# A decoder layer's last stage: the closing norms given behind the last expert's down product, and two late sums kept in weight slots

## The chip, the core and the metric

The kernel runs on one core of one Trainium2 chip. The metric is the device time of one execution in microseconds; the number shown is the median of three runs. A core has five instruction queues that concern us: TensorE (PE in the rows), VectorE (DVE), ScalarE (ACT), GpSimd (POOL) and SyncE (SP). SP issues the plain DMA transfers, POOL issues the indirect ones (gathers and scatters of rows by a list of indices), and both run on the core's 16 DMA engines. Every engine takes its own instructions strictly in the order in which they stand.

## The reference, cut to what matters

One decoder layer over 1024 tokens of width 1024 (T = D = 1024), in float32: parallel token mixing, cross-attention, and then a mixture of 16 experts, each sublayer followed by a layer norm. Only the end of it matters here:

```python
y = grouped_moe(x, router_w, router_bias, moe_w_gate[l], moe_w_up[l], moe_w_down[l])
x = layer_norm(DN_ALPHA * x + y, ln3_g[l], ln3_b[l])

# in grouped_moe, for a block xb of 128 tokens of expert e
(jax.nn.silu(xb @ w_gate[e]) * (xb @ w_up[e])) @ w_down[e]
# every token has two experts; their outputs are weighted by the gate and summed per token
```

## The kernel before

`Experts.run` does the 16 experts, `NE = 16`, in an order that is drawn up at run time: eight of them (a fixed first one and the seven fullest) with a second, smaller block of up to 64 rows, and the emptiest two (`LATE = 2`) last. By place in that order they are experts 0 to 15 here, so 14 and 15 are the late ones, and expert 13 is the last that has a second block. An expert gathers 128 token rows (`gather`), turns them (`turned`), and multiplies them by its gate, up and down weights. All products are float32 in three passes: each operand is split into a high and a low part (`split`, line 28, and `parts`, lines 1533 and 1534: ACT writes the high part, DVE the low one) and `mm3` (lines 35 to 37) makes three matmuls of it. The products land in the PSUM banks `eacc`, the turned tokens in `etp`, the split hidden row block in `ehh` and `ehl`.

`accd` (`self.acc`) is a table in device memory of one row per token. It starts as the residual, already divided by the layer's factor, and every expert adds its weighted rows `ey` to it with an indirect DMA that accumulates (line 1642). The last layer norm turns it into the output, in two ways:

- **The tiles.** `tiles` loads the 1024 rows of `accd` as 8 tiles of 128 tokens (line 1778, on SP's queue, into four slots that otherwise hold raw weights, `wraw`, two tiles in a slot), takes the mean and variance of each (`moments`: on DVE by line 980, two instructions a tile, for tiles 0, 1 and 7; on ACT by lines 974 and 975 for tiles 2 to 6), gets the reciprocal root on POOL (lines 976, 982 and 983), applies them in two passes of DVE over 128x1024 (`apply`, lines 989 and 994), and stores each tile to `out` (line 1784).
- **The late experts.** Experts 14 and 15 don't wait for that. Each gathers its tokens' rows from `accd` into a buffer `z` (named `exg`), adds its own weighted down product to it on DVE (line 1639, one instruction for each half of the width), norms `z` in the same way, and scatters the finished rows to `out` over those that the tiles have written (line 1645). It also adds its rows to `accd`, since expert 15 may hold a token of expert 14, and since a loop behind the experts (`rest`, which does nothing with these inputs) reads `accd` again.

The experts are generators with four steps: turn the tokens, gate product, up product, down product with the outputs. `run` interleaves them; in round n it gives the gate product of expert n, then the down product of n-1, then the turning of n+1, then the up product of n. In round 15 the tiles stand between the first two:

```python
            step(n)
            if n == NE - LATE + 1:
                ...
                x = [self.piece("raw").rearrange("p (a b) c -> p a (b c)", a=2) for _ in range(HOLD)]
                self.tiles([x[t // 2][:, t % 2] for t in range(2 * HOLD)])
            step(n - 1)
```

That order is not yet the order on the engines. The program goes through a scheduler with a timing model of its own, which sets the order of every engine's queue and keeps the dependences; what is given earlier tends to come earlier. What one operation needs of another becomes a wait on a semaphore. DMAs of POOL signal on eight of them in turn, DMASW0 to DMASW7; those of SP on DMAHW0 to DMAHW7.

Of the kernel before, what the change touches and what calls it, by code (L numbers as in the profile page):

```python
# [7 lines left out]
F32 = mybir.dt.float32  # L8
# [3 lines left out]
ALU = mybir.AluOpType  # L12
# [1246 lines left out]
FIRST = (14, 6, 6, 6, 6, 6, 6, 7)  # L1259
HOLD = 4  # L1260
CUT, LOPOOL = 4, ()
LATE = 2
# [214 lines left out]
class Experts:  # L1477
# [20 lines left out]

    def piece(self, kind):
        s = self.slots[kind]  # L1500
        pool, tag = s[self.n[kind] % len(s)]
        self.n[kind] += 1
        return pool.tile([128, 4, 512], F32 if kind == "raw" else F32R, tag=tag, bufs=1, name="w" + kind)

# [9 lines left out]

    def load(self, e, i):
        a = self.k.a
        raw = self.piece("raw")
        w = a["moe_w_" + ("gate", "up", "down")[i // 2]][0]
        w = w[e:e + 1] if isinstance(e, int) else w[bass.ds(e, 1)]
        if i < 4:  # L1520
            w = w.rearrange("o (h c p) n -> h p (o c) n", h=2, p=128)[i % 2]
        else:
            w = w.rearrange("o (c p) (h n) -> h p (o c) n", h=2, p=128)[i % 2]
        self.k.nc.sync.dma_start(raw, w)
        return raw

    def parts(self, raw):
        nc = self.k.nc
        hi, lo = self.piece("hi"), self.piece("lo")
        n = 4 // CUT  # L1530
# [42 lines left out]

    def expert(self, px, ps, w, main, rem, first=None, late=False):


        k, nc = self.k, self.k.nc
        xh, xl = first or (px.tile([128, 8, 128], F32R, tag=n, bufs=2, name=n) for n in ("exh", "exl"))
        for q in range(0 if first else 2):
            k.split(self.turned(ps, main[2], q).rearrange("p (c t) -> p c t", c=4), xh[:, 4 * q:4 * q + 4], xl[:, 4 * q:4 * q + 4])  # L1580
        yield
        wt = w(0)
        o = self.bank(ps)
        for c in range(8):
            hi, lo = wt[c // 4]
            k.mm3(o, xh[:, c], xl[:, c], hi[:, c % 4], lo[:, c % 4], c == 0, c == 7)
        th = px.tile([128, 512], F32, tag="th", bufs=2, name="eth")
# [20 lines left out]
        for c in range(8):  # L1608
            hi, lo = wt[c // 4]
            k.mm3(o, xh[:, c], xl[:, c], hi[:, c % 4], lo[:, c % 4], c == 0, c == 7)  # L1610
# [4 lines left out]
        hh, hl = (px.tile([128, 4, 128], F32R, tag=n, bufs=1, name=n) for n in ("ehh", "ehl"))  # L1615
        wt = w(2, k.split(self.turned(ps, th, 0).rearrange("p (c t) -> p c t", c=4), hh, hl))
        if rem:
# [9 lines left out]

        def result(tag, x, mm):
            y = px.tile([128, D], F32, tag="y" + tag, bufs=2 if tag == "m" else 1, name="ey")
            if late:  # L1630
                z = self.gather(px, x[0][:, 1:2], tag, self.acc)
            for d in range(2):
# [5 lines left out]
                if late:  # L1638
                    nc.vector.scalar_tensor_tensor(z[:, ds], o, x[1], z[:, ds], ALU.mult, ALU.add)  # L1639
            for r in ([slice(0, 128)] if tag == "m" else [slice(0, 64), slice(64, 128)]):  # L1640
                ix = x[0][0:r.stop - r.start, 1:2]
                nc.gpsimd.indirect_dma_start(out=self.acc, out_offset=bass.IndirectOffsetOnAxis(ap=ix, axis=0), in_=y[r, :], in_offset=None, compute_op=ALU.add, bounds_check=T - 1, oob_is_err=False)  # L1642
            if late:
                self.ln(z)
                nc.gpsimd.indirect_dma_start(out=self.out, out_offset=bass.IndirectOffsetOnAxis(ap=x[0][:, 1:2], axis=0), in_=z, in_offset=None, bounds_check=T - 1, oob_is_err=False)
        result("m", main, lambda o, f, hi, lo: k.mm3(o, hh[:, f], hl[:, f], hi[:, f], lo[:, f], f == 0, f == 3))
        if rem:
# [28 lines left out]
    def run(self, px, ps):  # L1676
# [41 lines left out]
        def step(n):  # L1718
            if 0 <= n < NE:
                if n == len(gens):  # L1720
                    gens.append(self.expert(px, ps, lambda i, after=(): pair(n, i, after), *toks[n], first=None if n else self.x0, late=n >= NE - LATE))
                next(gens[n])
        open_(0)
        gather(0, 1)
        step(0)
        open_(1)
        for n in range(NE + 1):
            if n == NE - LATE + 1:
                self.held = HOLD
            step(n)  # L1730
            if n == NE - LATE + 1:
                row = lambda tag: px.tile([128, D], F32, tag=tag, bufs=1, name="e" + tag)
                self.norm(self.pl, row("xgr"), row("exr"), [row("gr"), row("yr")])
# [7 lines left out]
            if n + 1 < NE:  # L1741
                gather(n + 1, 1)
    def ahead(self, experts=range(FIXED)):

        while self.at < 6 * NE and len(self.pre) < len(self.slots["raw"]) - self.held and self.seq[self.at][0] < len(experts):
            n, i = self.seq[self.at]
            self.pre.append(self.load(experts[n], i))
            self.at += 1
# [174 lines left out]
```

## Time and profile before

| | |
|---|---|
| median of 3 runs | 1833.93 us (1832.9 to 1838.39) |
| profiled execution, its own time | 1839.95 us |
| its span, first to last instruction | 1838.1 us |
| PE busy | 1724.6 us (94%) |
| DVE busy | 1228.9 us (67%) |
| ACT busy | 845.0 us (46%) |
| POOL busy | 434.3 us (24%) |
| mean granted clock of TensorE | 0.97 |

Times in the rows are microseconds from the span's start. "Busy" counts work only: an engine that waits, issues a DMA or branches isn't busy. The whole kernel is a TensorE kernel; the change touches its last 60 us, where TensorE runs out of work.

### The profile page before, as it was taken

What the parts mean: (1) busy time and instruction counts of PE and PEld (TensorE: products, weight loads), DVE (VectorE), ACT (ScalarE), POOL (GpSimd) and SP (SyncE); (2) the same over time, 40 slices, a digit from 0 to 9 for tenths busy, and PEclk for the clock granted to TensorE, in tenths of its full rate; (3) what the DMA queues carried; (4) which work ended last, traced back from release to release, by engine and by line L of the source; (5) the groups of instructions that cost most, each with busy time, mean ns of one, the idle gap of its engine ahead of it and who ended that gap; (6) DMA issues with size and microseconds to landing.
All of it is one profiled execution on the core that took longest, in us unless ns stands there. A gap on an engine that the chain in (4) does not pass through costs nothing. (4 is left out here: it accounts for less than half of the span.)

```text
span 1838.1 us, 27269 instructions
## 1 busy us (share of the span) xinstructions
PE 1724.6 (94%) x9254; PEld 1409.2 (77%) x9254; DVE 1228.9 (67%) x2821; ACT 845.0 (46%) x1756; POOL 434.3 (24%) x639
## 2 busy tenths in 40 slices
PE   8999989999999999999999889999996999999992
PEld 6877767877688878787887668778885888888871
DVE  4336766787875212698996865557866677777786
ACT  4233313444333221598885431043304667667672
POOL 0002101110110000366673221100033323333214
PEclk9999989999999999999999999999978999999996
DMA  7364344454333238602104745214415999989974
GB/s 239 112 186 131 110 150 130 133 169 135 107 95 91 86 97 246 206 10 93 33 12 133 232 154 172 72 29 149 161 47 187 307 299 297 294 294 306 312 273 151
DMA packets 252798, 295.96 MB, mean 161 GB/s; under 512 B 63789, under 2 KB 150981, under 8 KB 252144
## 3 DMA queue, kind: packets, MB, share of 16 engines
q1 hardware_dynamic: 245184, 273.52, 45.4%
q0 software_dynamic: 7472, 20.67, 4.6%
q8 instruction: 74, 1.21, 0.3%
q14 instruction: 68, 0.56, 0.1%
HBM read 231.88 MB, written 70.98 MB: 165 GB/s over the span
## 5 line engine op out<-in xcount | busy, mean ns | idle before, releaser
L35 PE MATMUL acc<-xh,wh 128*128 128x512 f32 (+1 forms) x656 | 269.6, 412 | 3.8 <-ACT ev L240 1.4
L36 PE MATMUL acc<-xl,wh 128*128 128x512 f32 (+1 forms) x656 | 265.2, 405 | 0.0
L37 PE MATMUL acc<-xh,wl 128*128 128x512 f32 (+1 forms) x656 | 264.6, 404 | 0.0
L1534 DVE TENSOR_TENSOR wlo<-wraw,whi 128x512 fp32r<-128x512 f32 x384 | 237.5, 684 | 32.6 <-ACT whi L1533 27.9
L1533 ACT CAST whi<-wraw 128x512 fp32r<-128x512 f32 x384 | 206.0, 621 | 19.1 <-issue 17.8
L35 PEld LDWEIGHTS acc<-xh,wh 128*128 128x128 f32 (+1 forms) x656 | 123.1, 188 | 39.2 <-issue 5.6
L37 PEld LDWEIGHTS acc<-xh,wl 128*128 128x128 f32 (+1 forms) x656 | 123.4, 188 | 33.8 <-issue 5.9
L36 PEld LDWEIGHTS acc<-xl,wh 128*128 128x128 f32 (+1 forms) x656 | 123.4, 188 | 32.1 <-issue 5.5
L477 ACT ACTIVATE pp<-pp,nm 128x640 f32<-128x640 f32 (+7 forms) x128 | 94.1, 738 | 8.2 <-DVE nm L476 6.5
L28 DVE TENSOR_TENSOR pl<-ptp,ph 128x512 fp32r<-128x512 f32 x132 | 87.9, 685 | 13.3 <-ACT ph L28 12.6
L120 DVE TENSOR_TENSOR wl<-wraw,wh 128x512 fp32r<-128x512 f32 (+1 forms) x82 | 52.8, 682 | 62.0 <-ACT wh L117 61.5
L35 PE MATMUL eacc<-whi,exh 128*128 128x512 f32 x240 | 94.2, 392 | 0.0
L36 PE MATMUL eacc<-wlo,exh 128*128 128x512 f32 x240 | 93.9, 391 | 0.0
L37 PE MATMUL eacc<-whi,exl 128*128 128x512 f32 x240 | 93.9, 391 | 0.0
L482 POOL TENSOR_SCALAR pp<-pp,wgt 128x640 f32<-128x640 f32 (+7 forms) x128 | 88.4, 711 | 0.6
L910 ACT COPY state<-rseq 64x64 f32<-64x64 f32 x128 | 26.6, 208 | 122.5 <-PE rseq L906 108.7
L28 ACT CAST ph<-ptp 128x512 fp32r<-128x512 f32 x132 | 74.3, 582 | 17.1 <-PE ptp L536 16.1
L536 PE MATMUL ptp<-ident,pp 128*128 128x128 f32 x528 | 79.8, 275 | 1.3 <-DVE pl L28 1.1
L1642 POOL DMA_INDIRECT accd<-ey,ef x32 | 52.1, 1628 | 115.2 <-ACT whi L1533 50.6
L852 DVE TENSOR_TENSOR tinv<-xinv,ln 128x60 f32<-128x60 f32 (+24 forms) x248 | 54.0, 218 | 32.8 <-DMA ln<-ld 27.0
L536 PEld LDWEIGHTS ptp<-ident,pp 128*128 128x128 f32 x528 | 64.5, 141 | 14.6 <-DVE pl L28 2.8
L467 PE MATMUL sp<-nk,nq 128*128 128x320 f32 (+5 forms) x192 | 71.9, 377 | 3.6 <-DVE nm L476 2.1
(497 smaller groups left out, 4291.0 us busy)
## 6 DMA issues: line engine op xcount, KB each, us to landing
wraw<-in_moe_w_up SPq DMA_DIRECT2D x32, 1024.0 KB
wraw<-in_moe_w_gate SPq DMA_DIRECT2D x32, 1024.0 KB
wraw<-in_moe_w_down SPq DMA_DIRECT2D x32, 1024.0 KB
wraw<-in_w_in SPq DMA_DIRECT2D x40, 512.0 KB
sm<-ev SPq DMA_DIRECT2D x32, 256.0 KB
sr<-ev SPq DMA_DIRECT2D x28, 256.0 KB
skew<-skew SPq DMA_DIRECT2D x1, 4608.0 KB
xraw<-in_x SPq DMA_DIRECT2D x8, 512.0 KB
```

Of the source, the lines that this page charges most:

```text
L28: x = nc.scalar.copy(hi, src), (nc.gpsimd if by_pool else nc.vector).tensor_tensor(lo, src, hi.bitcast(F32), ALU.subtract)
L35: nc.tensor.matmul(out, ah, bh, start=start, stop=False)
L36: nc.tensor.matmul(out, ah, bl, start=False, stop=False)
L37: nc.tensor.matmul(out, al, bh, start=False, stop=stop)
L120: nc.vector.tensor_tensor(wl[:, cs], raw[:, cs], wh[:, cs].bitcast(F32), ALU.subtract)
L467: nc.tensor.matmul(sp[:, o], t["q"][:, i, qs], t["k", br, "h"][:, kk], start=True, stop=False)
L477: nc.scalar.activation(pt[:, :n], pt[:, :n], AF.Exp, bias=nm, scale=-1.0, accum_out=sums[:, 0, i:i + 1])
L482: nc.gpsimd.tensor_scalar(st[br, i][:, :n], st[br, i][:, :n], w[:, 0, i:i + 1], 1.0, ALU.mult, ALU.mult)
L536: nc.tensor.transpose(tp[:, 128 * i:128 * i + 128], st[br, i][:, c0:c0 + 128], ident)
L852: nc.vector.tensor_tensor(tmp[:, :m, :w], x[:, :m, j:j + 1].to_broadcast([128, m, w]), ln[:, j:j + 1, j + 1:].to_broadcast([128, m, w]), A ...
L1533: nc.scalar.copy(hi[:, cs], raw[:, cs])
L1534: (nc.gpsimd if i in LOPOOL else nc.vector).tensor_tensor(lo[:, cs], raw[:, cs], hi[:, cs].bitcast(F32), ALU.subtract)
```

## The change

In round 15, `run` now only makes the norm's tiles of constants and calls a new helper `fetch(0)`, which gathers expert 14's rows of `accd` into half of a raw weights' slot. The tiles are given after all rounds, behind expert 15's down product. Expert 14 adds its rows to `accd` as before and then calls `fetch(1)` for the other half of the slot; the scatters of both late experts to `out`, and expert 15's addition to `accd`, are collected in `self.ends` and given after the tiles. The late sums so live in a `wraw` slot in place of `exg`. The diff also brings a variant `plain` of the experts, which `PLAIN = 0` switches off (`n >= NE - 0` is never true); its branches are left out below.

```diff
         def result(tag, x, mm):
+            add = lambda r: nc.gpsimd.indirect_dma_start(out=self.acc, out_offset=bass.IndirectOffsetOnAxis(ap=x[0][0:r.stop - r.start, 1:2], axis=0), in_=y[r, :], in_offset=None, compute_op=ALU.add, bounds_check=T - 1, oob_is_err=False)
             y = px.tile([128, D], F32, tag="y" + tag, bufs=2 if tag == "m" else 1, name="ey")
             if late:
-                z = self.gather(px, x[0][:, 1:2], tag, self.acc)
+                z = self.sums.pop(0)
...
-            for r in ([slice(0, 128)] if tag == "m" else [slice(0, 64), slice(64, 128)]):
-                ix = x[0][0:r.stop - r.start, 1:2]
-                nc.gpsimd.indirect_dma_start(out=self.acc, ...)
             if late:
+                n = len(self.ends)
+                if n < LATE - 1:
+                    add(slice(0, 128))
+                    self.fetch(n + 1)
+                self.ends.append(lambda: nc.gpsimd.indirect_dma_start(out=self.out, out_offset=bass.IndirectOffsetOnAxis(ap=x[0][:, 1:2], axis=0), in_=z, in_offset=None, bounds_check=T - 1, oob_is_err=False))
                 self.ln(z)
-                nc.gpsimd.indirect_dma_start(out=self.out, ...)
+                if n == LATE - 1:
+                    self.ends.append(lambda: add(slice(0, 128)))
+            else:
+                for r in [slice(0, 128)] if tag == "m" else [slice(0, 64), slice(64, 128)]:
+                    add(r)
...
+        def fetch(i):
+
+            if i % 2 == 0:
+                self.pair = self.piece("raw").rearrange("p (a b) c -> p a (b c)", a=2)
+            z = self.pair[:, i % 2]
+            nc.gpsimd.indirect_dma_start(out=z, out_offset=None, in_=self.acc, in_offset=bass.IndirectOffsetOnAxis(ap=toks[NE - LATE + i][0][0][:, 1:2], axis=0))
+            self.sums.append(z)
+        self.fetch, self.sums, self.ends = fetch, [], []
...
             step(n)
             if n == NE - LATE + 1:
+                self.fetch(0)
                 row = lambda tag: px.tile([128, D], F32, tag=tag, bufs=1, name="e" + tag)
                 self.norm(self.pl, row("xgr"), row("exr"), [row("gr"), row("yr")])
-                x = [self.piece("raw").rearrange("p (a b) c -> p a (b c)", a=2) for _ in range(HOLD)]
-                self.tiles([x[t // 2][:, t % 2] for t in range(2 * HOLD)])
-            step(n - 1)
+                step(n - 1)
+            else:
+                step(n - 1)
             step(n + 1)
...
+        x = [self.piece("raw").rearrange("p (a b) c -> p a (b c)", a=2) for _ in range(HOLD)]
+        self.tiles([x[t // 2][:, t % 2] for t in range(2 * HOLD)])
+        for end in self.ends:
+            end()
```

Up to expert 15's up product the queues of all engines read as before. Three places differ that the next sections speak of. The first is DVE's queue, from the up product of expert 15 (`eth`, its gated product) on. Before (`wraw` rows are tiles, `exg` rows the late sums):

```order
L1611 SCALAR_TENSOR_TENSOR eth<-eth,eacc 128x512
L989 SCALAR_TENSOR_TENSOR wraw<-wraw,lnmv,exgr 128x1024 x3
L994 SCALAR_TENSOR_TENSOR wraw<-wraw,lnrs,eexr 128x1024
L1639 SCALAR_TENSOR_TENSOR exg<-eacc,ef,exg 128x512
L994 SCALAR_TENSOR_TENSOR wraw<-wraw,lnrs,eexr 128x1024
L980 BN_STATS lnst<-wraw 128x6 x2
L989 SCALAR_TENSOR_TENSOR wraw<-wraw,lnmv,exgr 128x1024
L1639 SCALAR_TENSOR_TENSOR exg<-eacc,ef,exg 128x512
L994 SCALAR_TENSOR_TENSOR wraw<-wraw,lnrs,eexr 128x1024
L28 TENSOR_TENSOR ehl<-etp,ehh 128x512
```

And now, from the first half of expert 14's sum on (the line numbers of the changed kernel: 1656 is the sum, 1627 the gated product; sums and tiles are both called `wraw`, the first four `wraw` rows and the two norm passes are expert 14's, then come both halves of expert 15's sum, and the six statistics are expert 15's two and tiles 0 and 1's four):

```order
L1656 SCALAR_TENSOR_TENSOR wraw<-eacc,ef,wraw 128x512
L980 BN_STATS lnst<-wraw 128x6
L1656 SCALAR_TENSOR_TENSOR wraw<-eacc,ef,wraw 128x512
L1627 SCALAR_TENSOR_TENSOR eth<-eth,eacc 128x512
L980 BN_STATS lnst<-wraw 128x6
L981 BN_AGGR lnmv<-lnst 128x2
L989 SCALAR_TENSOR_TENSOR wraw<-wraw,lnmv,exgr 128x1024
L28 TENSOR_TENSOR ehl<-etp,ehh 128x512
L994 SCALAR_TENSOR_TENSOR wraw<-wraw,lnrs,eexr 128x1024
L1656 SCALAR_TENSOR_TENSOR wraw<-eacc,ef,wraw 128x512 x2
L980 BN_STATS lnst<-wraw 128x6 x6
L981 BN_AGGR lnmv<-lnst 128x2 x3
```

All work on tiles moved behind both halves of expert 15's sum, and the low part `ehl` of expert 15's hidden rows moved ahead of all of it. Behind these rows stand 18 passes of lines 989 and 994 (expert 15's two and the tiles' 16), tile 7's statistics and their aggregation, and nothing else.

The second place is POOL's queue of DMAs around expert 14's addition, with its waits. Before (the first row is expert 13's last addition, the second gathers expert 14's rows; the third is expert 14's addition, which stands behind several norm instructions left out here):

```order
L1642 DMA accd<-ey,ef 1152x1024 [waits DMASW4_49,DMASW3_49]
L1561 DMA exg<-accd,ef 128x1024 [waits DMASW4_49,PE_49]
...
L1642 DMA accd<-ey,ef 1152x1024 [waits DMAHW3_49,DMAHW4_49,DMAHW2_49,DMAHW5_49,DMAHW1_49,DMAHW6_49,DMAHW0_49,DMAHW7_49,DMASW5_49,Activation_49]
...
L1561 DMA exg<-accd,ef 128x1024 [waits DMASW6_49,DMASW0_49,PE_49]
...
L1642 DMA accd<-ey,ef 1152x1024 [waits DMASW7_49,Activation_49]
...
L1645 DMA out<-exg,ef 1024x1024 [waits DMAHW4_49,DMAHW3_49,DMAHW5_49,DMAHW2_49,DMAHW6_49,DMAHW1_49,DMAHW7_49,DMAHW0_49,DVE_49]
...
L1645 DMA out<-exg,ef 1024x1024 [waits DMASW1_49,DVE_49]
```

And now (the fourth row gathers expert 15's rows):

```order
L1645 DMA accd<-ey,ef 1152x1024 [waits DMASW4_49,DMASW3_49]
L1751 DMA wraw<-accd,ef 128x1024 [waits DMAHW4_49,DMAHW5_49,DMASW4_49,DVE_49]
L1645 DMA accd<-ey,ef 1152x1024 [waits DMASW5_49,Activation_49]
...
L1751 DMA wraw<-accd,ef 128x1024 [waits DMASW6_49]
...
L1645 DMA accd<-ey,ef 1152x1024 [waits DMAHW3_49,DMAHW4_49,DMAHW2_49,DMAHW5_49,DMAHW1_49,DMAHW6_49,DMAHW0_49,DMAHW7_49,DMASW7_49,DMASW0_49]
...
L1662 DMA out<-wraw,ef 1024x1024 [waits DMAHW4_49,DMAHW5_49,DMAHW3_49,DMAHW6_49,DMAHW2_49,DMAHW7_49,DMAHW1_49,DMAHW0_49]
L1662 DMA out<-wraw,ef 1024x1024 [waits DMASW1_49]
```

The wait for all eight tile loads (DMAHW0 to DMAHW7) moved from expert 14's addition to expert 15's. Before, the scatters had norm instructions between them; now both stand last, the first behind the eight tile stores, the second behind the first. In both kernels expert 13's last addition signals on DMASW4, the gather behind it on DMASW5, and expert 14's addition on DMASW6, which the gather of expert 15's rows waits for.

The third place is SP's queue, where the eight tile loads begin. Before:

```order
L1778 DMA wraw<-accd 128x1024 [waits DMAHW5_49,DMASW4_49,DVE_49]
L1778 DMA wraw<-accd 128x1024
L1778 DMA wraw<-accd 128x1024 [waits DMAHW6_49,DVE_49]
L1778 DMA wraw<-accd 128x1024 [waits DMAHW7_49]
L1778 DMA wraw<-accd 128x1024 [waits DMAHW0_49,DVE_49]
```

And now:

```order
L1815 DMA wraw<-accd 128x1024 [waits DMAHW6_49,DMASW6_49,DVE_49]
L1815 DMA wraw<-accd 128x1024 [waits DMAHW5_49]
L1815 DMA wraw<-accd 128x1024 [waits DMAHW0_49,DVE_49]
L1815 DMA wraw<-accd 128x1024 [waits DMAHW7_49]
L1815 DMA wraw<-accd 128x1024 [waits DMAHW1_49,DVE_49]
```

The first load's wait moved from DMASW4, expert 13's last addition to `accd`, to DMASW6, expert 14's. On TensorE one thing moved: the last six matmuls of expert 15's up product stood ahead of the last twenty of expert 14's down product and now stand behind them.

## Rows read from the trace of the kernel before

**Rows 1.** The head of the page.

```profile
span 1838.1 us, 27269 instructions
```

**Rows 2.** Busy time of the engines in five stretches near the end: the stretch, its length, then PE, PEld, DVE, ACT and POOL busy us (and instructions), the granted clock of TensorE, the share of the DMA engines, GB/s.

```profile
1795.00:1800.00 5.00, 2.08 (x4) 1.17 (x4) 5.00 (x6) 5.00 (x11) 4.58 (x5) 0.58 0.19 78
1800.00:1805.00 5.00, 0.04 (x1) 0.05 (x1) 5.00 (x8) 0.82 (x2) 0.68 (x2) 0.50 0.92 220
...
1820.00:1825.00 5.00, 0.00 (x0) 0.00 (x0) 2.52 (x4) 0.00 (x0) 1.89 (x3) 0.50 0.32 128
1825.00:1830.00 5.00, 0.00 (x0) 0.00 (x0) 0.86 (x1) 0.00 (x0) 1.06 (x1) 0.50 0.29 114
1830.00:1838.00 8.00, 0.00 (x0) 0.00 (x0) 0.00 (x0) 0.00 (x0) 0.00 (x0) 0.50 0.00 1
```

**Rows 3.** The chain of work that ended last, in order of time: start, us, what.

```profile
1777.26 2.77 DMA accd<-ey,ef
...
1780.09 3.50 DMA wraw<-accd
...
1822.53 3.38 DMA out<-exg,ef
```

**Rows 4.** Timeline of DVE: start, us, engine, line, operation, out<-in, count, and in brackets the idle time before with what ended it.

```profile
1783.61 1.29 DVE L980 BATCH_NORM_STATS2 lnst<-wraw 128x6 f32<-128x512 f32 x2 [1.47 <-DMA wraw<-accd]
...
1793.34 3.67 DVE L989 SCALAR_TENSOR_TENSOR wraw<-wraw,lnmv,exgr 128x1024 f32<-128x1024 f32 x3
...
1798.12 0.75 DVE L1639 SCALAR_TENSOR_TENSOR exg<-eacc,ef,exg 128x512 f32<-128x512 f32 x1
...
1804.21 0.69 DVE L28 TENSOR_TENSOR ehl<-etp,ehh 128x512 fp32r<-128x512 f32 x1
...
1810.86 2.47 DVE L994 SCALAR_TENSOR_TENSOR wraw<-wraw,lnrs,eexr 128x1024 f32<-128x1024 f32 x2
...
1820.60 0.21 DVE L981 BATCH_NORM_AGGREGATE lnmv<-lnst 128x2 f32<-128x12 f32 x1
1820.84 1.28 DVE L989 SCALAR_TENSOR_TENSOR exg<-exg,lnmv,exgr 128x1024 f32<-128x1024 f32 x1
1824.57 1.28 DVE L994 SCALAR_TENSOR_TENSOR exg<-exg,lnrs,eexr 128x1024 f32<-128x1024 f32 x1 [2.45 <-POOL lnrs L983]
```

**Rows 5.** Timeline of PE, same columns: the end of expert 15's up product (`exl`), the last twenty matmuls of expert 14's down product (first and last of them), the turning of expert 15's hidden rows, the first of expert 15's down product, the first one that needs `ehl`, and the last.

```profile
1788.25 0.39 PE L37 MATMUL eacc<-whi,exl 128*128 128x512 f32 x1
1788.47 0.40 PE L37 MATMUL eacc<-whi,ehl 128*128 128x512 f32 x1
...
1792.91 0.40 PE L37 MATMUL eacc<-whi,ehl 128*128 128x512 f32 x1
1793.48 0.66 PE L1568 MATMUL etp<-ident,eth 128*128 128x128 f32 x4 [0.17 <-DVE eth L1611]
1796.52 0.80 PE L35 MATMUL eacc<-whi,ehh 128*128 128x512 f32 x1 [2.39 <-ACT ehh L28]
...
1804.96 0.80 PE L37 MATMUL eacc<-whi,ehl 128*128 128x512 f32 x1 [6.36 <-DVE ehl L28]
...
1811.52 0.40 PE L37 MATMUL eacc<-whi,ehl 128*128 128x512 f32 x1
```

**Rows 6.** Timeline of ACT, same columns: the two halves of expert 14's weighted rows, and the high part of expert 15's hidden rows.

```profile
1792.15 0.67 ACT L1637 ACTIVATE ey<-eacc,ef 128x512 f32<-128x512 f32 x1
...
1795.33 0.67 ACT L1637 ACTIVATE ey<-eacc,ef 128x512 f32<-128x512 f32 x1
1795.90 0.57 ACT L28 CAST ehh<-etp 128x512 fp32r<-128x512 f32 x1
```

**Rows 7.** Timeline of POOL, same columns: an addition of expert 13 (64 rows), the gather of expert 14's rows, the additions of expert 14 and of expert 15 (128 rows each), and the two scatters to the output.

```profile
1774.30 1.42 POOL L1642 DMA_INDIRECT accd<-ey,ef  x1 [7.50 <-ACT whi L1533]
...
1780.81 0.99 POOL L1561 DMA_INDIRECT exg<-accd,ef  x1 [2.08 <-PE eacc L37]
...
1797.60 2.16 POOL L1642 DMA_INDIRECT accd<-ey,ef  x1 [0.18 <-ACT eyr L974]
...
1813.94 2.13 POOL L1642 DMA_INDIRECT accd<-ey,ef  x1 [0.18 <-issue]
...
1822.53 1.08 POOL L1645 DMA_INDIRECT out<-exg,ef  x1 [4.68 <-DVE exg L989]
...
1826.71 1.06 POOL L1645 DMA_INDIRECT out<-exg,ef  x1 [2.17 <-DVEq L1755]
```

**Rows 8.** Timeline of SP's queue: the eight tile loads.

```profile
1780.09 3.82 SPq L1778 DMA_DIRECT2D wraw<-accd  x8
```

**Rows 9.** DMA queues in five stretches, as packets, MB and share of the 16 engines; q1 carries SP's transfers, q0 POOL's. In this order: 1781 to 1785 us (only q1 moved anything), 1785 to 1788.2 us, 1793 to 1794 us (none of q1 behind it until 1798), 1800 to 1804.1 us (q0 alone shown, expert 14's addition), 1816 to 1820 us (q0 alone shown, expert 15's addition).

```profile
q1 hardware_dynamic: 357, 1.33, 97.9%
...
q1 hardware_dynamic: 232, 0.83, 63.6%
q0 software_dynamic: 144, 0.52, 40.1%
...
q1 hardware_dynamic: 28, 0.05, 13.2%
...
q0 software_dynamic: 143, 0.45, 72.3%
...
q0 software_dynamic: 144, 0.44, 70.3%
```

More of the change, by code (lines that the diff above doesn't have):

```diff
@@ L1572, in bank, with expert, turned, product @@
         return ps.tile([128, 512], F32, tag="acc", bufs=5, name="eacc")
-    def expert(self, px, ps, w, main, rem, first=None, late=False):
+    def expert(self, px, ps, w, main, rem, first=None, late=False, plain=False):
         k, nc = self.k, self.k.nc
-        xh, xl = first or (px.tile([128, 8, 128], F32R, tag=n, bufs=2, name=n) for n in ("exh", "exl"))
+        def turned(x, q, h, l):
+            tp = self.turned(ps, x, q).rearrange("p (c t) -> p c t", c=4)
+            if plain:
+                i = nc.scalar.copy(h[:, 0:2], tp[:, 0:2]), nc.vector.tensor_copy(h[:, 2:4], tp[:, 2:4])
+                return [j.ins for j in i]
+            return k.split(tp, h, l)
+        def product(o, h, l, w, i, n):
+            if plain:
+                nc.tensor.matmul(o, h[:, i], w[0], start=i == 0, stop=i == n - 1)
+            else:
+                k.mm3(o, h[:, i], l[:, i], *w, i == 0, i == n - 1)
+        xh, xl = first or (px.tile([128, 8, 128], F32 if plain else F32R, tag=n, bufs=2, name=n) for n in ("exh", "exl"))
         for q in range(0 if first else 2):
-            k.split(self.turned(ps, main[2], q).rearrange("p (c t) -> p c t", c=4), xh[:, 4 * q:4 * q + 4], xl[:, 4 * q:4 * q + 4])
+            turned(main[2], q, xh[:, 4 * q:4 * q + 4], xl[:, 4 * q:4 * q + 4])
         yield
@@ L1584, in expert @@
         for c in range(8):
-            hi, lo = wt[c // 4]
-            k.mm3(o, xh[:, c], xl[:, c], hi[:, c % 4], lo[:, c % 4], c == 0, c == 7)
+            product(o, xh, xl, [x[:, c % 4] for x in wt[c // 4]], c, 8)
         th = px.tile([128, 512], F32, tag="th", bufs=2, name="eth")
@@ L1608, in expert @@
         for c in range(8):
-            hi, lo = wt[c // 4]
-            k.mm3(o, xh[:, c], xl[:, c], hi[:, c % 4], lo[:, c % 4], c == 0, c == 7)
+            product(o, xh, xl, [x[:, c % 4] for x in wt[c // 4]], c, 8)
         nc.vector.scalar_tensor_tensor(th, th, 0.5, o, ALU.mult, ALU.mult)
@@ L1614, in expert @@
         yield
-        hh, hl = (px.tile([128, 4, 128], F32R, tag=n, bufs=1, name=n) for n in ("ehh", "ehl"))
-        wt = w(2, k.split(self.turned(ps, th, 0).rearrange("p (c t) -> p c t", c=4), hh, hl))
+        hh, hl = (px.tile([128, 4, 128], F32 if plain else F32R, tag=n, bufs=1, name=n) for n in ("ehh", "ehl"))
+        wt = w(2, turned(th, 0, hh, hl))
         if rem:
@@ L1720, in step @@
                 if n == len(gens):
-                    gens.append(self.expert(px, ps, lambda i, after=(): pair(n, i, after), *toks[n], first=None if n else self.x0, late=n >= NE - LATE))
+                    gens.append(self.expert(px, ps, lambda i, after=(): pair(n, i, after), *toks[n], first=None if n else self.x0, late=n >= NE - LATE, plain=n >= NE - PLAIN))
                 next(gens[n])
+        def fetch(i):
[5 more added lines that the diff above has]
+        self.fetch, self.sums, self.ends = fetch, [], []
         open_(0)
```

18 lines of the change are left out of this document (10 added, 8 removed).

## The prediction

> **What bounds the kernel now.** I read the chain that ended last first. Its last 58 us run from expert 13's last addition to `accd` [rows 3], which lands at 1780.03 (1777.26 + 2.77), over the first tile load (3.50 us) into a long stretch of DVE, and end in the two scatters to the output. The stretches [rows 2] say why DVE: from 1795 to 1805 it is busy all 10 us, while PE has 2.1 us of work, because PE waits. PE's own rows [rows 5] show for what: expert 15's down product starts at 1796.52 and stops for 6.36 us until 1804.96, released by `ehl`. ACT had the high part ready at 1796.5 (1795.90 + 0.57) [rows 6], and DVE came to the low part only at 1804.21 [rows 4], since norm passes of the tiles stood ahead of it. So up to 1783.6 TensorE sets the time, and from there to its last pass (1824.57 + 1.28 = 1825.85) DVE does, with almost no idle time: 1.47 us before the first tile's statistics and 2.45 us before the last pass. Behind that come only the second scatter, issued at 1826.71 [rows 7], and 11.4 us to the end of the span, in the last 8 of which no engine is busy [rows 2].
>
> The reader should see that DVE's tail is not late because it works on the wrong things, but because it has some 40 us of work that can begin at 1783.6 at the earliest, when the first tile is there.
>
> **The change part by part.** It removes next to nothing: the same tiles, sums, gathers and scatters are issued. It moves them, and four steps of the move stand on the path to the end.
>
> *When the tile loads may start.* They read `accd`. Before, they stood ahead of expert 14's addition and waited for expert 13's. Now they stand behind it, and the first load waits for it. So the addition has to be timed. PE runs the same matmuls in the same time, but expert 15's last six up matmuls stand behind the down product now; at 0.23 us from one to the next (from 1788.47 to 1792.91 for 19 steps) [rows 5] the down product ends 1.4 us earlier, at 1793.3 - 1.4 = 1791.9. ACT then needs 0.67 us for the second half [rows 6] with no norm ahead of it: 1792.6, and POOL issues the addition at about 1792.7, against 1797.60 [rows 7]. From issue to the last packet the two additions of 128 rows took 1797.60 to about 1804.1 (6.5 us) and 1813.94 to about 1819.7 (5.8 us) [rows 7, 9]. POOL's own part was 2.1 us in both; the 64-row addition at a quieter time took 1.42 us. The bounds are 5.0 (5.8 less the 0.7) and 6.5; I take 5.7, near the second row. The addition lands at 1798.4, and the tile loads start there: 18.3 us later than at 1780.09 [rows 8].
>
> *When expert 15's sum is there.* The gather of its rows waits for the same addition, so POOL issues it at the same moment as SP the loads. DVE has both halves of this sum ahead of every tile's statistics in its queue, so no tile work starts before it. What does the gather take? Expert 14's gather was issued at 1780.81 [rows 7], 0.72 us behind the first of eight tile loads [rows 8], and its 144 packets moved between 1785 and 1788.1; from 1781 to 1785 the loads alone moved [rows 9]. That is 7.2 us from issue. The lower bound is an indirect transfer of the same rows with nothing beside it, 3.38 us [rows 3]. The upper is that it waits out all the loads, which took 13.1 us (1780.09 to about 1793.2) [rows 8, 9], and then moves in some 1.5 us: 14.6. The row that is nearest, eight tile loads issued together with a gather, gives 7.2, and I take that: 1805.6. [...]
>
> [...]
>
> *What DVE does from there.* Between expert 14's norm, done by about 1798, and 1805.6 it has nothing it may do. This is the new stall, some 7.5 us, and with shorter waits for expert 14's halves it holds about 10. Behind it stand 2 halves of the sum, 8 statistics, 4 aggregations and 18 passes. Start to start: a half 0.66 (1798.12, 0.75 long with some 0.09 of overlap), a statistic 0.60 (two in 1.29), a pass 1.19 (two in 2.47 less one of 1.28), an aggregation 0.11 [rows 4]. That is 1.3 + 4.8 + 0.4 + 21.4 = 27.9 us. The sum begins at 1805.8, so the last pass ends at 1833.7, against 1825.85: 7.9 us later. The tiles themselves are hidden in this: all are landed 13.1 us after the first issue, at 1811.5, when DVE is at its second or third pass. ACT's statistics and POOL's roots for tiles 2 to 7 keep ahead too: expert 15's addition waits on POOL for the last load and costs 2.2 us there, and tile 3's root behind it is wanted some 10 us later. If they didn't, each late root would stop DVE by what the 2.45 us row shows [rows 4].
>
> *What stands behind the last pass.* Before, the tile stores and the first scatter were hidden by DVE's work, and only the second scatter came behind. Now the last pass is a tile's: its store, the first scatter behind it and the second behind that are a chain. For the store I take 3.4 us, between the tile load's 3.50 and the scatter's 3.38 of the same size [rows 3] (bounds 2.8, the addition's 2.77, and 5.4, were it as slow as store and wait together before). From first to second scatter 1822.53 to 1826.71 gives 4.2 us [rows 7]. The second scatter is issued at 1833.7 + 3.4 + 4.2 = 1841.3, against 1826.71: 14.6 us later. The 11.4 us behind it stay.
>
> What is gained costs nothing and gives nothing: PE's 6.4 us stall goes, but expert 15's product waits for the gather then. Buffers in weight slots are free by then, and their place changes no duration.
>
> **The sum.** The profiled execution took 1839.95 us and its span 1838.1 [rows 1]; with 14.6 more that is 1854.6 and 1852.7. It is 6 us above the median of the three runs, and all terms lie in the tail, so I add them to the median: 1833.93 + 14.6 = 1848.5. With the low bounds (addition -0.7, gather -3.8, store -0.6) it is +9.5, with the high ones (+0.8, +7.4, +2.0) +24.8.
>
> **The rivals.**
> [...]
> - *The gather waits out the loads*: +22.0, 1855.9 us. Against it speaks that the gather before did get in between.
> - *The last 8 us hide it.* Nothing is busy in them [rows 2], so what they wait for may run beside the tail already. Then up to 8.1 of the 14.6 vanish: +6.5, 1840.4. Against it: it lies behind the last scatter.
> - *Faster: the late expert, not the tiles, sets the end.* DVE held expert 15's low part back for 7.7 us (1796.5 to 1804.21); if the end hung on that expert, the time would fall by that, to 1826. The point from which it decides: the 27.9 us block would have to begin before 1805.8 - 14.6 = 1791.2, that is before expert 14's down product is even finished. Only if the tile loads didn't wait for expert 14's addition, and tiles could fill DVE's gaps, would that be so; the queues say that they do and can't.
>
> **How the numbers follow.** Chances: my sum 0.54, shared gather 0.22, gather last 0.13, hidden end 0.06, faster 0.05. The runs of before spread over 0.3%, 5.5 us, so that is the bound of "same". The first three and half of the fourth are slower: 0.92. The rest of the fourth and a little of the fifth are the same, 0.04, and faster is 0.04. The predicted time is 1848.5; the range of 1842 to 1857 leaves out the last two cases and the worst of the late gather, some 0.15.
>
> **What would show it.** Right: expert 14's addition issued near 1792.7; tile loads at about 1798, not 1780; DVE idle for 5 to 9 us ahead of expert 15's sum (line 1656), released by the gather; no stop of PE for `ehl`; DVE's last pass on a tile; and store, scatter, scatter as the last chain. Wrong: tile loads before 1795, DVE busy without a gap from 1798 on, or a last scatter before 1835.

## The result and the profile after

The changed kernel is slower, by about one per cent. In the first timing its median is 1856.3 us over 5 runs (1849.42 to 1859.07), beside 1834.65 us over 5 runs of the kernel before; the ratio is 1.0100, with a 95% interval of 1.0076 to 1.0124. A second timing gave 1850.27 us over 6 runs beside 1836.36 us over 29: 1.0076 (1.0056 to 1.0095). The forecast was 1848.5 us, in a range of 1842 to 1857, with slower at 0.92. The first median lies only 0.7 us under the upper end of that range, and two of its five executions lie above it (1859.03 and 1859.07); the second lies near the forecast.

> The changed kernel once more. If its tail is a property of the order and not of one execution, a second profile gives 73 to 75 us from the first matmul of expert 14's down product to the end, and the timed difference to before should come near the difference of the tails, 17.9 us or 1.0%. If the medians differ by 21 us or more again, something ahead of the tail costs the rest.

The profiled execution took 1849.42 us. Its page begins:

```profile
span 1847.6 us, 27270 instructions
```

**How executions are compared.** All that differs lies in the last 75 us, but what comes ahead of them is not equally long in every execution: the first matmul of expert 14's down product, which both kernels reach over the same work, starts at 1781.95 us before and at 1773.56 after. So I measure from that matmul (the anchor) to the end of the span and call it the tail. Before, it is 1838.1 - 1781.95 = 56.15 us; after, 1847.6 - 1773.56 = 74.04, which is 17.9 more; in the profile of the second timing it is 1846.7 - 1771.02 = 75.68, a little above the 73 to 75 that were expected of it. The medians of the two timings differ from the kernel before by 21.7 and 13.9 us, and the differences of the tails, 17.9 and 19.5, lie between these. Four stretches of the tail after, cut at the first tile load, at the start of expert 15's sum on DVE and at the end of DVE's last pass, and a fifth that lies within the fourth (columns as in [rows 2]):

```profile
1773.56:1790.48 16.92, 15.22 (x65) 11.72 (x66) 12.39 (x19) 6.08 (x11) 3.46 (x3) 1.00 0.28 58
1790.48:1798.64 8.16, 2.88 (x13) 1.99 (x11) 0.00 (x0) 1.77 (x3) 1.11 (x1) 0.93 0.86 325
1798.64:1828.59 29.95, 0.00 (x0) 0.00 (x0) 28.36 (x32) 10.92 (x20) 22.13 (x19) 0.50 0.58 207
1828.59:1847.60 19.01, 0.00 (x0) 0.00 (x0) 0.00 (x1) 0.00 (x0) 2.07 (x2) 0.50 0.19 76
1838.80:1847.60 8.80, 0.00 (x0) 0.00 (x0) 0.00 (x0) 0.00 (x0) 0.00 (x0) 0.50 0.03 11
```

The same cuts for before are its first tile statistic, 1783.61, and the end of its last pass, 1825.85:

```profile
1781.95:1783.61 1.66, 1.66 (x7) 1.39 (x8) 0.19 (x2) 1.66 (x4) 0.00 (x0) 1.00 0.93 378
1783.61:1825.85 42.24, 19.39 (x70) 14.37 (x69) 39.76 (x50) 16.77 (x30) 23.11 (x24) 0.73 0.69 238
1825.85:1838.10 12.25, 0.00 (x0) 0.00 (x0) 0.01 (x1) 0.00 (x0) 1.06 (x1) 0.50 0.10 37
```

The reader should see two things. Before, DVE's 40 us of work in the tail ran nearly without a gap from 1.66 us behind the anchor; after, 12.4 us of it stands ahead of an 8.2 us stretch in which DVE does nothing, and 28.4 behind. (The rows of DVE's queue in the section on the change start at 1792.74 in before. Ahead of them, from 1783.61 [rows 4] on, DVE had already done the first two tiles' four statistics, two aggregations and a first pass; these moved behind expert 15's sum as well.) DVE's last pass ends 1825.85 - 1781.95 = 43.90 us behind the anchor before and 1828.59 - 1773.56 = 55.03 after: 11.1 us. And behind that pass come 19.0 us instead of 12.25: 6.8. The two make the 17.9.

What DVE waited for, and what it ran from there, in its timeline (answers to [rows 4]):

```profile
1788.58 1.28 DVE L994 SCALAR_TENSOR_TENSOR wraw<-wraw,lnrs,eexr 128x1024 f32<-128x1024 f32 x1 [0.19 <-POOL lnrs L983]
1798.64 1.41 DVE L1656 SCALAR_TENSOR_TENSOR wraw<-eacc,ef,wraw 128x512 f32<-128x512 f32 x2 [8.79 <-DMA wraw<-accd,ef]
...
1808.22 1.28 DVE L994 SCALAR_TENSOR_TENSOR wraw<-wraw,lnrs,eexr 128x1024 f32<-128x1024 f32 x1 [0.65 <-POOL lnrs L983]
...
1824.36 1.28 DVE L994 SCALAR_TENSOR_TENSOR wraw<-wraw,lnrs,eexr 128x1024 f32<-128x1024 f32 x1 [0.44 <-POOL lnrs L983]
...
1827.31 1.28 DVE L994 SCALAR_TENSOR_TENSOR wraw<-wraw,lnrs,eexr 128x1024 f32<-128x1024 f32 x1 [0.46 <-POOL lnrs L983]
```

POOL's timeline: expert 14's addition, the gather of expert 15's rows, norm roots of tiles (lines 976, 982 and 983), and the two scatters (answers to [rows 7]):

```profile
1784.51 1.57 POOL L1645 DMA_INDIRECT accd<-ey,ef  x1 [11.60 <-ACT ey L1654]
...
1790.70 1.11 POOL L1751 DMA_INDIRECT wraw<-accd,ef  x1 [2.16 <-DMA accd<-ey,ef]
1803.96 3.68 POOL L982 TENSOR_SCALAR lnrs<-lnmv 128x1 f32<-128x1 f32 x3 [12.16 <-DVE lnmv L981]
...
1825.81 1.46 POOL L983 TENSOR_TENSOR lnrs<-lnrs,ln3h 128x1 f32<-128x1 f32 x1
1832.65 1.09 POOL L1662 DMA_INDIRECT out<-wraw,ef  x1 [5.38 <-SPq L1792]
1836.30 0.98 POOL L1662 DMA_INDIRECT out<-wraw,ef  x1 [2.56 <-DMA out<-wraw,ef]
```

SP's queue: the eight tile loads (answers to [rows 8]) and the eight tile stores:

```profile
1790.48 3.94 SPq L1815 DMA_DIRECT2D wraw<-accd  x8
1811.93 17.02 SPq L1821 DMA_DIRECT2D out<-wraw  x8
```

PE: the anchor, and the first matmul that needs `ehl`, for which PE stopped 6.36 us before [rows 5] and now 0.24:

```profile
1773.56 0.50 PE L35 MATMUL eacc<-whi,ehh 128*128 128x512 f32 x1 [0.73 <-ACT ehh L28]
...
1788.44 0.50 PE L37 MATMUL eacc<-whi,ehl 128*128 128x512 f32 x1 [0.24 <-DVE ehl L28]
```

### The profile page after: what moved, and what is told of

Same layout as the page of the kernel before. It is cut to its first block, busy times and chain, and to the rows that moved or that the text cites. A ratio compares the mean times of both kernels' runs of the same rounds, so it can differ in the third digit from the quotient of the medians.

```text
span 1847.6 us, 27270 instructions
## 1 busy us (share of the span) xinstructions
PE 1716.9 (93%) x9254; PEld 1405.1 (76%) x9254; DVE 1228.8 (67%) x2821; ACT 844.9 (46%) x1756; POOL 436.7 (24%) x639
## 5 line engine op out<-in xcount | busy, mean ns | idle before, releaser
L1537 ACT CAST whi<-wraw 128x512 fp32r<-128x512 f32 x384 | 206.0, 621 | 18.8 <-issue 17.4
L28 DVE TENSOR_TENSOR pl<-ptp,ph 128x512 fp32r<-128x512 f32 x132 | 87.9, 686 | 13.1 <-ACT ph L28 12.4
```

The costliest lines, as they stand in the source:

```text
L28: x = nc.scalar.copy(hi, src), (nc.gpsimd if by_pool else nc.vector).tensor_tensor(lo, src, hi.bitcast(F32), ALU.subtract)
L1537: nc.scalar.copy(hi[:, cs], raw[:, cs])
```

## The experiments

Each started from the changed kernel unless it says otherwise. The theory under test is the prediction's: the tiles' passes stand in DVE's queue behind expert 15's sum, and that sum waits for a chain, addition of expert 14, then gather; DVE idles, and at the end the store of a tile and two scatters follow one another. The time beside each run is that of the kernel before, timed together with it: 1834.2 us over 16 executions for the first four runs, 1836.36 over 29 for the last three. The tails are of one profile each, and the two of the changed kernel differ by 1.6 us. The rivals: the late tile loads alone are the cost; the slots and the collected scatters cost something themselves; PE's old stall was worth something.

### The tile loads early, the norms still late

```diff
                 self.norm(self.pl, row("xgr"), row("exr"), [row("gr"), row("yr")])
+                x = [self.piece("raw").rearrange("p (a b) c -> p a (b c)", a=2) for _ in range(HOLD)]
+                xs = [x[t // 2][:, t % 2] for t in range(2 * HOLD)]
+                for t in range(2 * HOLD):
+                    nc.sync.dma_start(xs[t], self.acc[128 * t:128 * t + 128, :])
...
-        x = [self.piece("raw").rearrange("p (a b) c -> p a (b c)", a=2) for _ in range(HOLD)]
-        self.tiles([x[t // 2][:, t % 2] for t in range(2 * HOLD)])
+        self.tiles(xs, loaded=True)
```

> The changed kernel, but the eight tile loads are given where the kernel before gave them, ahead of expert 14's down product; only the norms and stores of the tiles stay last. The measure is the tail: from the first matmul of expert 14's down product to the end of the span, 56.1 us before (1781.95 to 1838.1) and 74.0 us after (1773.56 to 1847.6). Theory A, DVE's queue starts its block of 28 to 30 us when expert 15's gathered rows are there, whatever the tiles do: the loads no longer stand beside that gather, so it takes some 4 us from issue, not 7.9; the addition of expert 14 waits for the loads to land and is issued some 0.5 us later; the block starts 3 to 4 us earlier and the tail is 69 to 71 us. Theory B, the loads' start, 18 us later relative to PE's work, is by itself what the change costs: then the tail returns to 56 to 59 us.

Measured: 1850.0 us beside 1834.2, a ratio of 1.0082 (1.0056 to 1.0108); the tail is 1845.9 - 1774.08 = 71.8 us, just above the 69 to 71 of theory A and far from the 56 to 59 of theory B. POOL, and DVE's wait for the gather:

```profile
1787.10 1.57 POOL L1645 DMA_INDIRECT accd<-ey,ef  x1 [13.14 <-issue]
...
1793.12 1.10 POOL L1751 DMA_INDIRECT wraw<-accd,ef  x1 [3.48 <-DMA accd<-ey,ef]
```

```profile
1797.69 0.75 DVE L1656 SCALAR_TENSOR_TENSOR wraw<-eacc,ef,wraw 128x512 f32<-128x512 f32 x1 [6.73 <-DMA wraw<-accd,ef]
```

The loads began at 1772.26, 1.8 us ahead of the anchor and so more than 18 us earlier against it than after, and only 2.2 of the lost 17.9 us came back. Late loads alone are not the cost. DVE still stood still for 6.7 us, for the same gather. The run also measures the gather with no load beside it: 1793.12 to 1797.69, 4.57 us, where it took 1790.70 to 1798.64, 7.94, after. Over half of that gain is paid back by expert 14's addition, issued 13.02 us behind the anchor instead of 10.95, where 0.5 us was expected. Its rows were ready as early as after (ACT at 1784.76, 10.68 us behind the anchor); the loads moved packets until about 1786, and the addition writes what they read, so the loads are the likely cause, though the profile names none.

### The tiles back where they were, slots and scatters as after

```diff
                 self.norm(self.pl, row("xgr"), row("exr"), [row("gr"), row("yr")])
+                x = [self.piece("raw").rearrange("p (a b) c -> p a (b c)", a=2) for _ in range(HOLD)]
+                self.tiles([x[t // 2][:, t % 2] for t in range(2 * HOLD)])
...
-        x = [self.piece("raw").rearrange("p (a b) c -> p a (b c)", a=2) for _ in range(HOLD)]
-        self.tiles([x[t // 2][:, t % 2] for t in range(2 * HOLD)])
         for end in self.ends:
```

> The changed kernel with the tiles, loads and norms, given where the kernel before gave them; the late sums stay in a weights' slot, the scatters and expert 15's addition stay collected at the end. If the loss is all in where the tiles stand, the tail is that of the kernel before, 56 us (55 to 58), and the time is within 0.3% of it. If the slots or the collected scatters cost something by themselves (a slot that comes free late, a scatter that waits longer), the tail is above 58.

Measured: 1834.75 us beside 1834.2, 1.0002 (0.9982 to 1.0021); tail 1832.9 - 1775.71 = 57.2 us, against 56.15 before. POOL's scatters stand as before's do, the first one under DVE's last passes:

```profile
1817.31 1.08 POOL L1662 DMA_INDIRECT out<-wraw,ef  x1 [4.97 <-DVE wraw L989]
...
1821.50 1.06 POOL L1662 DMA_INDIRECT out<-wraw,ef  x1 [2.17 <-DVEq L1792]
```

So the raw slots and the collected scatters cost 1 us at most, less than two profiles of one kernel differ. The loss goes with where the tiles stand, loads and norms; the loads alone gave back 2.2 us of it. PE has its stop for `ehl` back in this run (7.24 us), and it is as fast as before.

### Expert 15's gather ahead of expert 14's addition

```diff
                 self.fetch(0)
+                self.fetch(1)
...
-                    self.fetch(n + 1)
```

> The changed kernel with expert 15's gather given beside expert 14's, ahead of expert 14's addition. It leaves out that a token of both late experts gets expert 14's part in expert 15's row. If the 8.8 us in which DVE waited for that gather are on the path, they shrink to the wait for tile 0 (its load is issued at the same place, and landed 3.5 us behind it before): DVE starts on tile 0 some 3.5 us after the first load, about 4.5 us earlier than the 8.2 us now, and one half of the sum and its statistics are done by then: the tail is 67 to 69 us instead of 74. If the block waits for the tiles all the same (tiles 1 and 2 land late, ACT's statistics hold it), the tail is 72 or more.

Measured: 1845.21 us beside 1834.2, 1.0054 (1.0028 to 1.0080); tail 1844.2 - 1775.58 = 68.6 us. DVE:

```profile
1793.87 0.75 DVE L1656 SCALAR_TENSOR_TENSOR wraw<-eacc,ef,wraw 128x512 f32<-128x512 f32 x1 [1.95 <-ACT ey L1654]
...
1796.31 2.57 DVE L980 BATCH_NORM_STATS2 lnst<-wraw 128x6 f32<-128x512 f32 x4 [0.96 <-DMA wraw<-accd]
```

The 8.8 us of standing still became 1.95 + 0.96, and the tail is 5.4 us shorter than after. This is the wait on the chain of addition and gather, priced by taking it away. Of the 12.5 us of loss that are left, 6.7 lie behind DVE's last pass (1844.2 - 1825.21 = 18.99, against 12.25 before). The other 5.7 lie ahead of it: tile work still stands behind expert 15's sum, which now waits for that expert's own product (1.95, until 18.3 us behind the anchor), and the first tile's load still waits for expert 14's addition (0.96).

### Expert 14's and 15's rows to a table of their own

```diff
-                self.ends.append(lambda: nc.gpsimd.indirect_dma_start(out=self.out, ...
+                self.ends.append(lambda: None)
                 self.ln(z)
+                nc.gpsimd.indirect_dma_start(out=self.own, ...
```

> The changed kernel with both late experts' finished rows scattered to a table of their own as soon as they are ready; it leaves out that they overwrite their rows in the output. What is left behind DVE's last pass is one tile store. If the closing chain store, scatter, scatter is the second half of the loss, the two scatters go from the path: 3.65 us between them and as much for the second one, so the tail is 66 to 68 us. If something else of some 11 us stands behind the last pass whatever is scattered (the end of the program), the tail stays above 71.

Measured: 1846.28 us beside 1834.2, 1.0064 (1.0039 to 1.0088); tail 1845.1 - 1776.68 = 68.4 us, just above the 66 to 68 expected of the closing chain and under the 71 of its rival. The stretch behind the last pass (columns as in [rows 2]), and DVE's wait:

```profile
1834.27:1845.10 10.83, 0.00 (x0) 0.00 (x0) 0.00 (x1) 0.00 (x0) 0.00 (x0) 0.50 0.13 51
```

```profile
1803.52 1.41 DVE L1657 SCALAR_TENSOR_TENSOR wraw<-eacc,ef,wraw 128x512 f32<-128x512 f32 x2 [10.49 <-DMA wraw<-accd,ef]
```

Without the two scatters behind the last pass, the end takes 10.8 us instead of 19.0: the two scatters cost 8.2 us there. The tail fell by 5.6 only, because DVE's start of the sum and its block came later by 2.6 together. That the early scatter to the table, issued 1.4 us behind the gather, slowed the gather (9.6 us here, 7.9 after) is possible but not shown: the second profile of the changed kernel has 9.6 too.

### The kernel before, with all tiles' statistics on ACT

```diff
-BYACT, ADDV = (2, 3, 4, 5, 6), (0, 1, 2, 3, 4, 5, 6, 7)
+BYACT, ADDV = (0, 1, 2, 3, 4, 5, 6, 7), (0, 1, 2, 3, 4, 5, 6, 7)
```

> The kernel before, with the statistics of tiles 0, 1 and 7 on ACT as well, so that DVE does none. The tail (first matmul of expert 14's down product to the end of the span) was 56.1 us before. If DVE's sum of work sets the end of the kernel before, as the prediction had it, DVE loses six statistics and three aggregations, 3.9 us, and the tail falls by 2 to 4 us, to 52 to 54. If the end hangs on expert 15's chain (its product, gather and norm) or on POOL, the tail stays within 1 us of 56; if ACT's 2.5 us a tile become the bound, it grows.

Measured: 1832.08 us over 12 runs beside 1836.36 over 29, 0.9973 (0.9956 to 0.9990); tail 1831.8 - 1778.03 = 53.8 us, within the 52 to 54 expected. The tail as one stretch, of before and then of this run:

```profile
1781.95:1838.10 56.15, 21.05 (x76) 15.76 (x76) 39.96 (x51) 18.43 (x33) 24.17 (x25) 0.68 0.57 199
```

```profile
1778.03:1831.80 53.77, 21.28 (x76) 15.88 (x76) 36.65 (x42) 24.54 (x45) 27.63 (x25) 0.69 0.59 204
```

DVE has 3.3 us less to do and the tail is 2.4 us shorter. Together with the stretch of before in which DVE is busy for 39.76 of 42.24 us, this is what a tail bounded by DVE looks like. By itself the run doesn't tell DVE's sum of work from the chain of expert 15, because with less ahead of it in DVE's queue `ehl` came earlier too, at 19.6 us behind the anchor instead of 22.3, and PE's stop for it shrank from 6.36 us:

```profile
1798.35 0.80 PE L37 MATMUL eacc<-whi,ehl 128*128 128x512 f32 x1 [1.66 <-DVE ehl L28]
```

It is a version that beats both kernels, by a quarter of a per cent over before: little, but clear of the noise.

### The low part first, then tiles, then expert 15's sum

The loads are early as in the first experiment; `ehl` is made ahead of the tiles; expert 15's sum comes behind them, and only its scatter stands behind the loop.

```diff
                     nc.sync.dma_start(xs[t], self.acc[128 * t:128 * t + 128, :])
+                step(n - 1)
...
         wt = w(2, turned(th, 0, hh, hl))
+        if late:
+            yield
...
+            if n == NE - LATE + 1:
+                step(n)
+                self.tiles(xs, loaded=True)
+                self.ends[0]()
+        for end in self.ends[1:]:
```

> The changed kernel in another order: tile loads ahead of expert 14's down product, expert 15's hidden rows split right behind its up product, then the tiles' norms, then expert 14's scatter, and expert 15's sum, norm and scatter last. DVE has tiles to work on while expert 15's gather is under way, and only one scatter is left behind its last pass. If the loss of the change is DVE's idle time ahead of that sum and the two extra steps in the last chain, the tail comes back from 74 to 55 to 59 us. PE's 6.4 us stall of the kernel before is gone here too: if that stall was worth something, the tail is clearly under 56, about 50; if DVE was the bound all the time, it isn't. If late tile loads or POOL's queue (the gather waits there ahead of the tiles' roots) cost as much again, it stays above 62.

Measured: 1842.74 us over 12 runs beside 1836.36, 1.0025 (1.0009 to 1.0042); tail 1840.9 - 1779.02 = 61.9 us, above the 55 to 59 of the theory and just under the 62 of its last rival. POOL:

```profile
1791.52 1.56 POOL L1647 DMA_INDIRECT accd<-ey,ef  x1 [13.25 <-issue]
1798.15 1.46 POOL L1753 DMA_INDIRECT wraw<-accd,ef  x1 [5.06 <-DMA accd<-ey,ef]
...
1825.15 1.08 POOL L1664 DMA_INDIRECT out<-wraw,ef  x1 [1.54 <-SPq L1801]
1829.62 0.97 POOL L1664 DMA_INDIRECT out<-wraw,ef  x1 [3.38 <-DMA out<-wraw,ef]
```

PE no longer stops for `ehl`, and the kernel is not faster than before: the removal of PE's stall, which the change brought too, doesn't by itself make a kernel faster. What the stall alone is worth this run can't tell, since it changes the end too. The tail is 5.7 us longer than before's in two parts: the last pass ends 2.0 us later behind the anchor (45.91 against 43.90), and 3.7 us more follow it (15.97 against 12.25). For the first part, POOL's queue holds DVE up: the gather waits 5.06 us for the addition, and roots of tiles stand behind it (DVE waits 2.10 us for one). For the second, the first scatter goes out only behind the last tile store, 0.2 us behind DVE's last pass (1823.65 + 1.28 = 1824.93), so that one more scatter stands at the end than before, where the second scatter alone did [rows 7]: 1825.15 to 1829.62, 4.5 us.

### The same, with all statistics on ACT

```diff
-BYACT, ADDV = (2, 3, 4, 5, 6), (0, 1, 2, 3, 4, 5, 6, 7)
+BYACT, ADDV = (0, 1, 2, 3, 4, 5, 6, 7), (0, 1, 2, 3, 4, 5, 6, 7)
```

> As the one before, with the statistics of all eight tiles on ACT. If DVE's work is the bound in both, the tail falls by another 2 to 4 us, to 52 to 55 us, and the kernel is 0.1 to 0.3% faster than before. If POOL's wait for expert 14's addition or ACT's queue sets the pace, nothing is gained over the one before.

Measured: 1842.38 us over 12 runs beside 1836.36, 1.0033 (1.0014 to 1.0052); tail 1842.3 - 1779.52 = 62.8 us: a miss. Its tail as one stretch, and DVE's longest waits in it (us in total, times, longest):

```profile
1779.52:1842.30 62.78, 20.39 (x76) 15.42 (x76) 36.97 (x42) 24.75 (x45) 28.35 (x26) 0.69 0.51 179
```

```profile
DVE wraw L994 <- POOL lnrs L983: 5.8, 5, 2.5
```

DVE had 3 us less to do than in the run before (36.97 us against 40.16), but waited 5.8 us for POOL's roots instead of 2.9. The prediction took such roots to keep ahead in the changed kernel; the two longest, 2.50 and 1.94 us, are for roots that stood in POOL's queue behind expert 14's addition (1793.67) and behind the gather (1799.78), for which POOL itself waited 13.7 and 3.57 us:

```profile
1793.67 1.57 POOL L1647 DMA_INDIRECT accd<-ey,ef  x1 [13.68 <-ACT ehh L28]
...
1799.78 1.72 POOL L1753 DMA_INDIRECT wraw<-accd,ef  x1 [3.57 <-DMA accd<-ey,ef]
```

In the order of before the same edit gained; here, where DVE waits for POOL, it gave nothing. (PE's stop for `ehl` is back in this run, 4.03 us, since `ehl` stands behind the pass that waited 2.50 us.)

## Why the prediction was right, step by step

The direction, the mechanism and the place were right: the step that carries everything, that no tile work may start before expert 15's sum and that this sum hangs on addition and gather, is shown by the wait of 8.79 us, by the run with the tiles moved back (no loss) and by the one with the gather first (5.4 us back). The size was somewhat low: +14.6 forecast, +17.9 in the tail of the profile (19.5 in the second). Of the missing 3.3 us, 1.2 come before expert 15's sum begins, 2.05 are in DVE's block, and the end adds none. Each step; the first three rows as a distance from the anchor:

| step | forecast | measured |
|---|---|---|
| expert 14's addition issued | 1792.7 - 1781.95 = 10.75 | 10.95 |
| addition lands, tile loads begin | 16.45 | 16.92 |
| gather: issue to expert 15's sum | 7.2, sum at 23.85 | 7.94, sum at 25.08 |
| DVE's block, sum to last pass | 27.9 | 29.95 |
| last pass to first scatter (store) | 3.4 | 4.06 |
| first to second scatter | 4.2 | 3.65 |
| second scatter to the end | 11.4 | 11.3 |

**The addition and the loads.** Right within half a microsecond. (The forecast's lower bound, 5.8 less 0.7, is 5.1 and not 5.0, and it starts the sum 0.2 us behind the gather's 1805.6 without saying why; neither matters.) The loads' issue moved by 18.8 us against the anchor (16.92 behind it; before 1.86 ahead of it), and 18.3 was forecast.

**The gather.** It didn't wait for the loads, which ran on to about 1804 while expert 15's sum began at 1798.64, so that rival is false. Nor did it share from the start. The queues from 1791 to 1795 us, and from 1795 to 1798 (packets, MB, share, as in [rows 9]):

```profile
q1 hardware_dynamic: 308, 1.14, 81.7%
...
q1 hardware_dynamic: 194, 0.72, 58.6%
q0 software_dynamic: 143, 0.52, 42.7%
```

POOL was done with it at 1790.70 + 1.11 = 1791.81, and for over 3 us only loads moved, just as in [rows 9]; then the two shared. With no load beside it, in the run with the loads early, POOL was done at 1794.22 and the first packets moved before 1795, so the 3 us are not what a gather needs to start; no run here shows what held it back. PE did not hold the sum up: its last matmul of expert 15's product ended at 1793.36, 5.3 us ahead of it. The forecast by the nearest row, 7.2, was short by 0.7 in one profile and by 2.4 in the other (9.63): the term was sized well, but has some spread.

**DVE's block** is the term that was mis-sized most, by 2.05 us. The step that failed is "ACT's statistics and POOL's roots for tiles 2 to 7 keep ahead too". The counted work was right (DVE is busy 28.36 us of 29.95, and 27.9 was forecast), but DVE waited three times for a root, 0.65 + 0.44 + 0.46 = 1.55 us: once for the first root of the block, behind three small operations of POOL that stood ahead of it, and twice for roots of the last tiles, the last time on its very last pass. POOL ran from 1803.96 to 1827.3 nearly without a gap (22.13 us busy). Its rows show where the time went: three 128x1 operations took 3.68 us beside DVE's passes, and 0.61 in the run with the low part first, where DVE stood still. The last root took 1.46 us in after (row at 1825.81 above) and ended 0.42 us behind the pass of DVE in which it began (the first row below). In before a root took 0.57, both while DVE stood and waited for it and while DVE ran statistics. So the roots were longer where DVE's passes ran beside them; by what means no run here shows:

```profile
1825.57 1.28 DVE L989 SCALAR_TENSOR_TENSOR wraw<-wraw,lnmv,exgr 128x1024 f32<-128x1024 f32 x1
...
1799.98 1.28 DVE L980 BATCH_NORM_STATS2 lnst<-wraw 128x6 f32<-128x512 f32 x2
1800.20 0.57 POOL L983 TENSOR_TENSOR lnrs<-lnrs,ln3h 128x1 f32<-128x1 f32 x1
...
1823.64 0.24 POOL L982 TENSOR_SCALAR lnrs<-lnmv 128x1 f32<-128x1 f32 x1
1823.97 0.57 POOL L983 TENSOR_TENSOR lnrs<-lnrs,ln3h 128x1 f32<-128x1 f32 x1
```

The prediction had also misread what a late root costs. It took the 2.45 us row of before for that, but there expert 14's scatter stood ahead of the root in POOL's queue and was issued only at 1822.53 [rows 7]; the last two rows above, the root's two operations, follow it. A root that was late by POOL's own work cost 0.44 to 0.65 us.

**The end.** Store and scatters were each within 0.7 us, their sum within 0.1: 19.0 us in both. That the sum is so close is luck: the store was put 0.66 too low and the step between the scatters 0.55 too high. The rival that the last microseconds with no engine busy hide the chain is false; they only moved, behind the last scatter. The run without scatters at the end prices the two scatters at 8.2 us.

**PE's stall.** It went, as forecast, and the kernel became slower, so the rival that the late expert sets the end, and the time falls by its 7.7 us, is false for this change. The run with the low part first, in which the stall went too, is slower than before as well. No run takes only the stall away; what speaks against a worth of its own in before is that DVE stood idle there only twice, 1.47 us at the start and 2.45 at the end [rows 4].

**What stays open.** The timed difference was 21.7 us in one timing and 13.9 in the other, and the tail alone says 17.9 and 19.5. The rest is in what comes ahead of the tail, whose length in the profiles of all these kernels is 1771.0 to 1782.0 us; no run here tells what sets that. That the first difference comes out near the rival in which the gather waits out the loads (+22.0) is chance, since the trace shows that the gather didn't wait. And that its median still lies inside the forecast range is in part luck, since the forecast had terms in the tail only.

## What to carry to other kernels

Where an engine works through its queue in order and sets the end, ask of each move not how much work it holds but what now stands ahead of it and what that waits for: the tiles' statistics and passes, over 20 us that need nothing of the late experts, were put behind a sum of 1.4 us that had to wait for an addition to memory and a gather behind it. Look also at what follows the last pass: work that other passes hid (a store, a scatter) becomes a chain when the order turns, and cost here more than a third of the loss (6.8 of 17.9 us). And a stall on an engine that isn't the bound, PE's 6.4 us here, is by itself no reason to reorder; taking 3.3 us off DVE, the bound here, shortened the tail by 2.4.

## What the runs showed of the hardware

- A gather on POOL's queue that was issued beside eight loads of SP's got none of its packets for over 3 us after POOL was done with it, in before and in after. It took 7.2 us from issue to its last packet in before and 7.9 and 9.6 us from issue to use in the two profiles of after, and 4.57 from issue to use with no load beside it, where its packets began less than 1 us after POOL was done.
- In the tails of before and after, a 128x1 power on POOL (line 983) that stands in a row by itself took 0.55 to 0.57 us while DVE waited or ran statistics, and 1.45 to 1.49 us where it began while DVE ran its passes of 1.28 us. In DVE's block of 29.95 us in after, POOL was busy for 22.13, and DVE waited for its roots for 1.55.
- DVE took its instructions in the order of its queue: in the run with the loads early, where the loads moved packets until about 1786, it stood at expert 15's sum for 6.73 us, until 1797.69, with statistics of the tiles behind that sum.
- For the last 8.0 us before [rows 2] and 8.8 after no engine is busy, and next to nothing is transferred (1 and 11 GB/s). In these two kernels that stretch follows the last scatter. In the run with a table of its own, where the last transfer to `out` is a tile store, 10.83 us passed from DVE's last pass to the end of the span; less the 4.06 us that a store took behind the last pass in after, some 6.8 of them are such a stretch, by estimate.
